# The first 16 modulation blocks as TensorE matmuls in four column groups, and wide weight splits on VectorE

## The chip, the core and the metric

The kernel runs on one core of one Trainium2 chip. The metric is device time in microseconds (us). Three runs of the kernel before gave 1264.8, 1265.66 and 1267.31 us, median 1265.66 us.

The engines are named as in the profile: PE is TensorE's matmul, PEld its weight load, DVE is VectorE, ACT is ScalarE, POOL is GpSimd, SP the engine that issues most DMAs. L183 is line 183 of the kernel before.

## The reference, cut to what matters

One layer over 256 tokens of 1024 channels: a modulation from a conditioning vector, a mixer of three branches, and a mixture of 32 experts. What the change touches is the modulation:

```python
cond = silu(c)                                   # 1024 numbers
mod = cond @ w_ada + b_ada                       # 6 * 1024 numbers
sh_m, sc_m, g_m, sh_f, sc_f, g_f = split(mod, 6)
h = rms_norm(x, norm_mix) * (1 + sc_m) + sh_m    # [256, 1024]
proj = h @ w_in                                  # q, k, v, gates and so on
x = x + g_m * mixer(proj)
h = rms_norm(x, norm_ffn) * (1 + sc_f) + sh_f
x = x + g_f * moe_ffn(h)                         # 32 experts, top 4
```

`mod` is 48 blocks of 128 channels. The first 16 are `sc_m` and `sh_m`; nothing of `proj` can start on a block of 128 channels of `h` before its two blocks of `mod` are there.

## The kernel before, in words

**The first loop** (`branches`, eight passes, one for each block d of 128 channels). A pass loads two tiles `wada` of w_ada (512 KB each) and one tile `wt` of the q, k, v weights (`wqkv`, 896 KB). `ada` makes two columns of `mod`, each by one VectorE instruction (L183) that multiplies a [128, 1024] tile of w_ada, laid out with output channels on partitions, with silu(c) repeated on every partition (`csb`) and sums along the row. `h_chunk` then makes the scale (A, L214), the scaled and shifted block (hd, L217), its rounded part (the ACT cast, L218) and the rest (L219). The weights are split the same way (`split`): ACT rounds to `whi` (L103), POOL or DVE subtracts to get `wlo` (L95), in a wide piece of 1024 columns and one of 768. Three matmuls (`mm3`, L110 to L112) make one product: 24 matmuls in a pass, 18 of them with 512 columns and 6 with 256. Before, all splits of the loop but the last wide one are POOL's.

**silu(c) on every partition** is made by `row_tile` (L489): eight matmuls against the identity and two ACT copies, before the first pass.

**After the loop** come the norms of q and k (`qk_norm`, L275 to L289, on ACT, DVE and PE), the products of the other weights (`proj`, `proj_ch`), a chain of small DVE operations on [128, 4] (`lru_prepare`, sp, L297 to L313), differential attention, sliding-window attention, the recurrence (`lru`), and beside them the other 32 blocks of `mod` by the same VectorE instruction. Then the branches are merged, x is updated, tokens are routed, and the experts stream 12 MB of weights each.

**What sets the order.** Each engine runs its own list in order. The lists are written by a scheduler from the program's dependences and its own priorities, so an edit in the loop also changes the order behind it. Tiles come from pools: 9 tiles for `wada` and others (`p4`), 3 for `wt`, 3 each for `whi` and `wlo`, and 8 banks of PSUM, of which the loop holds 7 for its sums.

Of the kernel before, what the change touches and what calls it, by code (L numbers as in the profile page):

```python
# [27 lines left out]
# the blocks of 128 columns of mod, in the order in which they are computed  # L28
# [3 lines left out]
# those computed beside the chunks of the gates  # L32
ADA = [[10], [11], [12, 13], [14, 15], [16, 17], [18, 19], [20, 21], [22, 23], [], [], [], []]

# columns of the packed per-channel parameters
C_C, C_NM, C_NF, C_CW, C_CB, C_BA, C_BX, C_LAM = 0, 8, 16, 24, 40, 44, 48, 52
C_QG, C_KG, C_SG, C_SQ, C_SK, C_BADA, N_COLS = 56, 57, 58, 59, 60, 61, 109
# columns of the packed rows
R_SINK, R_BR, N_ROWS = 0, 8, 40
# columns of the packed constants  # L40
# [4 lines left out]
class Kernel:  # L45
# [11 lines left out]
    def mm(self):  # L57
        """A bank of PSUM for the products in turn: of two while the other two are held, or of four."""
        self.turn = (self.turn + self.four) % 2
        return self.po() if self.turn else self.psum.tile([128, 512], F32, name="mm", tag="mm", bufs=2)  # L60
# [7 lines left out]
    def weights(self, pool, bufs, after=0):  # L68
        """bufs more tiles for weights, to be used after the next few."""
# [13 lines left out]
    def load_pair(self, srcs):  # L83
        """Two blocks [128, 2, n] in one tile."""
# [6 lines left out]
    def sub_rest(self, lo, x, hi, eng=None):  # L91
        """lo = x - hi, what rounding x to hi has left."""
# [4 lines left out]
    def split(self, w, eng=None):  # L97
        """w as hi + lo, each exact in float32r."""
# [8 lines left out]
    def mm3(self, out, lhs, rhs, start, stop):  # L107
        """out += lhs.T @ rhs, both as (hi, lo)."""
# [52 lines left out]
    def silu_c(self):  # L161
        """Twice silu(c), on every partition."""
# [5 lines left out]
        self.csb = self.row_tile("silu", sc, self.mix)  # L168
        self.mod = self.keep.tile([128, 48], F32, name="mod")

    def ada_load(self, i, first=False):
        ws = []
        for j in range(2):
            ws.append(self.p4("wada") if first else self.p4p.tile([128, D], F32, name="wada", tag="wada", bufs=2))
            self.nc.sync.dma_start(out=ws[j], in_=self.a["wada"][i][:, j * D:(j + 1) * D])
        return ws

    def ada(self, i, ws=None):
        """Columns 2i and 2i + 1 of mod: two blocks of 128 channels."""
# [6 lines left out]
    def normed_T(self, out):  # L186
        """x, rms-normed and transposed, to out: two [128, 4, T]."""
# [21 lines left out]

    def h_chunk(self, x, d):  # L210
        """hhi + hlo [:, d] = channels 128d.. of h, transposed; x: those of normed_T."""
        nc = self.nc
        A = self.A1[:, d:d + 1]
        nc.vector.scalar_tensor_tensor(A, self.mod[:, 2 * d:2 * d + 1], 1.0, self.col(C_NM + d),  # L214
                                       op0=ALU.add, op1=ALU.mult)
# [6 lines left out]
    def bias_tiles(self):  # L222
        """tz[p, head, j]: minus the bias of distance p + j - 127, the masks included."""
# [17 lines left out]
    def tokens_k(self, ps, h, k, hi, lo):  # L241
        """ps[t] += h.T @ w for block k of the channels, w [128, 512] as hi + lo."""
# [4 lines left out]
    def proj(self, ps, h, src):  # L247
        """h.T @ w for 512 columns of w."""
# [11 lines left out]
    def proj_ch(self, i):  # L260
        """Two blocks of 128 channels [128, 2, tokens]."""
# [844 lines left out]
def layout(inp):  # L1106
# [3 lines left out]
    a = {}  # L1110
# [67 lines left out]
```

## Time and profile before

| | |
|---|---|
| median of three runs | 1265.66 us |
| span of the profiled execution | 1268.4 us |
| PE busy | 1136.3 us (90%) |
| DVE busy | 481.9 us (38%) |
| ACT busy | 254.6 us (20%) |
| POOL busy | 126.2 us (10%) |
| moved by DMA | 470.67 MB, mean 371 GB/s |

The page gives no time of the profiled execution but its span, which is 2.7 us above the median of the runs. Shares over the whole span mix stages that have different limits; the table of stages among the rows below keeps them apart. A row of the timeline reads: start, duration, engine, line, operation, result and operands, shapes, and in brackets how long the engine was idle before it and what ended that.

### The profile page before, as it was taken

What the parts mean: (1) busy time and instruction counts of PE and PEld (TensorE: products, weight loads), DVE (VectorE), ACT (ScalarE), POOL (GpSimd) and SP (SyncE); (2) the same over time, 40 slices, a digit from 0 to 9 for tenths busy, and PEclk for the clock granted to TensorE, in tenths of its full rate; (3) what the DMA queues carried; (4) which work ended last, traced back from release to release, by engine and by line L of the source; (5) the groups of instructions that cost most, each with busy time, mean ns of one, the idle gap of its engine ahead of it and who ended that gap; (6) DMA issues with size and microseconds to landing.
All of it is one profiled execution on the core that took longest, in us unless ns stands there. A gap on an engine that the chain in (4) does not pass through costs nothing.

```text
span 1268.4 us, 13945 instructions
## 1 busy us (share of the span) xinstructions
PE 1136.3 (90%) x5559; PEld 543.8 (43%) x5560; DVE 481.9 (38%) x864; ACT 254.6 (20%) x438; POOL 126.2 (10%) x62
## 2 busy tenths in 40 slices
PE   5798998899898899999899898989898989898997
PEld 4577878897334333433332232324232423332232
DVE  6979868774313232322123121303141312121232
ACT  4275647344201010100100000101010100100000
POOL 3643213442000000000000000000000000000000
PEclk8998989899899999999999999999999999999999
DMA  8668456688599999999999999999999999999996
GB/s 336 233 238 299 149 203 217 248 329 366 223 411 421 421 421 420 421 421 421 421 421 421 421 421 421 421 421 421 421 421 420 421 421 421 421 421 421 421 399 253
DMA packets 75084, 470.67 MB, mean 371 GB/s; under 512 B 8464, under 2 KB 10568, under 8 KB 23560
## 3 DMA queue, kind: packets, MB, share of 16 engines
q1 hardware_dynamic: 73544, 467.07, 90.9%
q0 software_dynamic: 464, 1.59, 0.4%
q10 hardware_dynamic: 1008, 1.09, 0.3%
q8 instruction: 45, 0.74, 0.2%
q14 instruction: 23, 0.19, 0.0%
HBM read 468.65 MB, written 1.07 MB: 370 GB/s over the span
## 4 chain that ended last, share of the span: by engine, by line
DMA 50%; PE 35%; DVE 12%; ACT 2%; issue 1%; ACTq 0%; SPq 0%; DVEq 0%
DMA wt<-w1h 30%; DMA wt<-w2h 18%; PE po L879 7%; PE mm L879 6%; PE ps L899 5%; DVE wada L183 4%; PE ps L839 2%; PE ps L912 2%; PE mm L112 2%; PE mm L110 2%; PE mm L111 2%; PE ps L383 1%; DVE wlo L95 1%; DVE A L214 1%; PE po L112 1%
## 5 line engine op out<-in xcount | busy, mean ns | idle before, releaser
L879 PE MATMUL po<-wt,xT 128*64 128x512 f32 x992 | 323.8, 605 | 34.5 <-DMA wt<-w1h 34.5
L879 PE MATMUL mm<-wt,xT 128*64 128x512 f32 x992 | 317.2, 596 | 0.0
L899 PE MATMUL ps<-wt,act 128*64 128x512 f32 x992 | 233.4, 607 | 28.6 <-DMA wt<-w2h 21.8
L905 DVE TENSOR_TENSOR y<-ps,gf 64x512 f32<-64x512 f32 x62 | 42.7, 689 | 380.8 <-PE ps L899 372.0
L879 PEld LDWEIGHTS po<-wt,xT 128*64 128x64 f32 x992 | 78.4, 136 | 176.9 <-DMA wt<-w1h 97.8
L879 PEld LDWEIGHTS mm<-wt,xT 128*64 128x64 f32 x992 | 88.4, 137 | 135.4 <-issue 134.6
L899 PEld LDWEIGHTS ps<-wt,act 128*64 128x64 f32 x992 | 68.2, 138 | 179.8 <-issue 122.2
L95 POOL TENSOR_TENSOR wlo<-wt,whi 128x1024 fp32r<-128x1024 f32 (+1 forms) x43 | 110.7, 2581 | 176.2 <-ACT whi L103 149.3
L809 DVE TENSOR_TENSOR g<-ps,b1t 128x512 f32<-128x512 f32 x31 | 21.4, 692 | 222.3 <-PE ps L806 222.3
L883 ACT COPY hg<-po 128x512 f32<-128x512 f32 x31 | 18.2, 586 | 361.5 <-PE po L879 315.4
L103 ACT CAST whi<-wt 128x1024 fp32r<-128x1024 f32 x72 | 72.7, 1022 | 55.2 <-PE mm L111 31.7
L183 DVE CUSTOM_DVE_ANT_0 wada<-wada,silu,cols 128x1024 f32<-128x1024 f32 x48 | 80.7, 1686 | 2.4 <-DMA wada<-wada 2.3
L112 PE MATMUL mm<-h,wlo 128*128 128x256 f32 x256 | 76.3, 298 | 5.8 <-DVE wlo L95 5.0
L110 PE MATMUL mm<-h,whi 128*128 128x256 f32 x256 | 77.2, 301 | 3.7 <-ACT gl L574 3.7
L111 PE MATMUL mm<-h,whi 128*128 128x256 f32 x256 | 76.5, 299 | 0.0
L912 PE MATMUL ps<-y,swT 128*128 128x512 f32 (+1 forms) x128 | 58.2, 606 | 11.2 <-DVE y L905 11.2
L812 ACT ACTIVATE ps<-g 128x512 f32<-128x512 f32 x31 | 18.6, 601 | 186.1 <-DVE g L810 186.1
L112 PEld LDWEIGHTS mm<-h,wlo 128*128 128x128 f32 x256 | 52.0, 203 | 7.3 <-DVE wlo L95 5.2
L110 PEld LDWEIGHTS mm<-h,whi 128*128 128x128 f32 x256 | 52.2, 204 | 4.6 <-ACT gl L574 3.9
L111 PEld LDWEIGHTS mm<-h,whi 128*128 128x128 f32 x256 | 51.9, 203 | 2.0 <-issue 2.0
L914 DVE TENSOR_TENSOR x<-x,ps 128x512 f32<-128x512 f32 x64 | 43.9, 688 | 15.7 <-PE ps L912 15.7
L95 DVE TENSOR_TENSOR wlo<-wt,whi 128x1024 fp32r<-128x1024 f32 x29 | 39.4, 1360 | 19.5 <-ACT whi L103 19.5
(325 smaller groups left out, 1139.1 us busy)
## 6 DMA issues: line engine op xcount, KB each, us to landing
wt<-w1h SPq DMA_DIRECT2D x248, 1024.0 KB, 19.8
wt<-w2h SPq DMA_DIRECT2D x126, 1024.0 KB, 19.8
wada<-wada SPq DMA_DIRECT2D x48, 512.0 KB, 5.4
wt<-wch SPq DMA_DIRECT2D x16, 1024.0 KB, 5.2
wt<-w1h SPq DMA_DIRECT2D x16, 512.0 KB, 10.8
wt<-wqkv SPq DMA_DIRECT2D x8, 896.0 KB, 4.6
wt<-wbr SPq DMA_DIRECT2D x6, 1024.0 KB, 6.8
wt<-wout SPq DMA_DIRECT2D x4, 1024.0 KB, 14.0
```

The source lines that it names most:

```text
L95: eng.tensor_tensor(lo, x, hi.bitcast(F32), op=ALU.subtract)
L103: self.nc.scalar.copy(hi, w)
L110: nc.tensor.matmul(out, lhs[0], rhs[0], start=start, stop=False)
L111: nc.tensor.matmul(out, lhs[0], rhs[1], start=False, stop=False)
L112: nc.tensor.matmul(out, lhs[1], rhs[0], start=False, stop=stop)
L183: nc.vector.tensor_tensor_reduce(out=w, in0=w, in1=self.csb, scale=0.5, scalar=self.col(C_BADA + c), op0=ALU.mult, op1=ALU.add, accum_out= ...
L839: nc.tensor.matmul(p[:, i * 256:(i + 1) * 256], self.xs[j][:, t, d * 128:(d + 1) * 128], sel[:, t], start=(t + j == 0), stop=(t + j == 2))
L879: nc.tensor.matmul(p[64 * hf:64 * hf + 64], xT[:, k, i * CAP:(i + 1) * CAP], w[:, (2 * j + hf) * 512:(2 * j + hf + 1) * 512], start=(k == ...
L899: nc.tensor.matmul(py[rows[hf]], act[:, (k % 4) * 2 + k // 4, :], w[:, (2 * i + hf) * 512:(2 * i + hf + 1) * 512], start=(k == 0), stop=(k ...
L905: nc.vector.tensor_mul(self.y[r, hf], py[r], self.gf[r, hf * 512:(hf + 1) * 512])
L912: nc.tensor.matmul(p, swT[r, i, t * 128:(t + 1) * 128], self.y[r, hf], start=True, stop=True)
L914: nc.vector.tensor_add(self.x[:, t, s], self.x[:, t, s], p)
```

## The change

`ada` no longer serves the loop. `ada_rows` does: for each of the eight blocks of the contraction one matmul, with silu(c) of that block repeated 32 times as stationary operand and 256 columns of w_ada (both blocks of `mod`) as moving one, in the column group k % 4 of TensorE. The four groups' sums, each on 32 partitions, are copied to SBUF by ACT (`rd`), and two matmuls against a column with four ones (`pick`) add the four and turn them to partitions. One DVE instruction applies the factor 0.5 and the bias with its 1 folded in (`bm`), so that A becomes a plain product. w_ada of the loop is laid out anew (`wad0`). The row tile of silu(c), still needed by the other 32 blocks, is made after the loop. All wide splits of the loop go to DVE, the 768-column ones stay on POOL.

```diff
     def silu_c(self):
         ...
-        self.csb = self.row_tile("silu", sc, self.mix)
+        self.sc = sc
+        self.pick = self.early.tile([128, 1], F32, name="pick")
+        nc.vector.memset(self.pick, 0.0)
+        for j in range(4):
+            nc.vector.memset(self.pick[32 * j:32 * j + 1], 1.0)
+        self.bm = self.early.tile([128, 8, 2], F32, name="bm")
+        b = self.col(C_BADA, 16).rearrange("p (d s) -> p d s", s=2)
+        nc.vector.tensor_scalar(self.bm[:, :, 0], b[:, :, 0], 1.0, None, op0=ALU.add)
+        nc.vector.tensor_copy(self.bm[:, :, 1], b[:, :, 1])
...
+    def ada_rows(self, d, ws):
+        nc = self.nc
+        p = self.ps()
+        for k in range(8):
+            j = k % 4
+            nc.tensor.matmul(p[32 * j:32 * j + 32, :256], self.sc[:, k:k + 1].to_broadcast([128, 32]),
+                             ws[k // 4][:, j * 256:(j + 1) * 256], start=(k < 4), stop=(k >= 4))
+        r = self.mw.tile([128, 256], F32, name="rd")
+        nc.scalar.copy(r, p[:, :256])
+        for i in range(2):
+            nc.tensor.matmul(p[:, 256 + i:257 + i], r[:, i * 128:(i + 1) * 128], self.pick, start=True, stop=True)
+        m = self.mod[:, 2 * d:2 * d + 2]
+        nc.vector.scalar_tensor_tensor(m, p[:, 256:258], 0.5, self.bm[:, d], op0=ALU.mult, op1=ALU.add)
...
     def h_chunk(self, x, d):
-        nc.vector.scalar_tensor_tensor(A, self.mod[:, 2 * d:2 * d + 1], 1.0, self.col(C_NM + d),
-                                       op0=ALU.add, op1=ALU.mult)
+        nc.vector.tensor_mul(A, self.mod[:, 2 * d:2 * d + 1], self.col(C_NM + d))
...
     def branches(self, br, gl):
         ...
-            self.ada(d, w)
+            self.ada_rows(d, w)
             self.h_chunk(gl[d // 4][:, d % 4], d)
-            hi, lo = self.split(wt[:, :1024], nc.vector if d == 7 else nc.gpsimd)
+            hi, lo = self.split(wt[:, :1024], nc.vector)
...
             nc.scalar.copy(dv[:, t], p)
+        self.csb = self.row_tile("silu", self.sc, self.mix)
...
+    a["wad0"] = wa[:, 1::-1].reshape(8, 128, 2, 8, 128).transpose(3, 1, 0, 2, 4).reshape(8, 128, 2048)
```

The change moves instructions in three places that matter below. On PE, at the seam of two passes, the list before goes from the last matmuls of one pass straight to the next (`h_75` and `h_76` are the rounded part of h and its rest):

```order
L110 MATMUL ps<-whi,h_75 128x256
L111 MATMUL ps<-wlo,h_75 128x256
L112 MATMUL ps<-whi,h_76 128x256
L110 MATMUL mm<-whi,h_75 128x512
L111 MATMUL mm<-wlo,h_75 128x512
```

In the changed list the two pick matmuls of the next pass and the eight matmuls of the pass after it stand between:

```order
L110 MATMUL ps<-whi,h_75 128x256
L111 MATMUL ps<-wlo,h_75 128x256
L112 MATMUL ps<-whi,h_76 128x256
L231 MATMUL ps<-pick,rd 128x1 x2
L226 MATMUL ps<-wada,sc 32x256 x8
L110 MATMUL mm<-whi,h_75 128x512
L111 MATMUL mm<-wlo,h_75 128x512
```

The eight use the one bank of PSUM that the loop doesn't hold, so they also wait until DVE has read the pick's result.

On DVE, after the loop, the small operations of the recurrence's parameters (sp) stand before in one piece behind all the norms of q and k but the last two, which come after them:

```order
L227 TENSOR_TENSOR relb<-ps,relb 12x383
L301 TENSOR_SCALAR sp<-sp 128x4
L183 ISA wada,mod<-wada,silu,cols 128x1024
L183 ISA mod 128x1
L95 TENSOR_TENSOR wlo<-wt,whi 128x1024
L302 RECIPROCAL sp<-sp 128x4
L303 TENSOR_TENSOR sp<-sp 128x4
L304 TENSOR_TENSOR sp<-sp 128x4
L305 TENSOR_SCALAR sp<-sp 128x4
L307 SCALAR_TENSOR_TENSOR sp<-sp 128x4 x7
L95 TENSOR_TENSOR wlo<-wt,whi 128x1024
```

In the changed list (its lines are 24 higher) they begin behind the first of the eight norms (q, L307):

```order
L307 TENSOR_TENSOR q<-ps,rs_715 128x512
L303 TENSOR_REDUCE ss_729<-sq 128x8
L95 TENSOR_TENSOR wlo<-wt,whi 128x1024
L192 ISA wada,mod<-wada,silu,cols 128x1024
L192 ISA mod 128x1
L325 TENSOR_SCALAR sp<-sp 128x4
L326 RECIPROCAL sp<-sp 128x4
L327 TENSOR_TENSOR sp<-sp 128x4
L328 TENSOR_TENSOR sp<-sp 128x4
L329 TENSOR_SCALAR sp<-sp 128x4
L158 RECIPROCAL rs_731<-rt 128x8
L331 SCALAR_TENSOR_TENSOR sp<-sp 128x4
```

Five of the 32 later sums stand ahead of the first score before, eight in the changed list.

On DVE, in the recurrence, nine of these sums stand behind the first operation on the gated input (L338) before, six in the changed list (there L362). The end of that stretch before, from the last operation of the recurrence on:

```order
L352 SCALAR_TENSOR_TENSOR xc<-xc,ti 128x1024
L183 ISA wada,mod<-wada,silu,cols 128x1024
L183 ISA mod 128x1
L624 TENSOR_TENSOR wr<-wr,A_2444 128x256
L183 ISA wada,mod<-wada,silu,cols 128x1024
L183 ISA mod 128x1
L95 TENSOR_TENSOR wlo<-wt,whi 128x1024
L183 ISA wada,mod<-wada,silu,cols 128x1024
L183 ISA mod 128x1
L95 TENSOR_TENSOR wlo<-wt,whi 128x1024
```

And in the changed list:

```order
L376 SCALAR_TENSOR_TENSOR xc<-xc,ti 128x1024
L192 ISA wada,mod<-wada,silu,cols 128x1024
L192 ISA mod 128x1
L95 TENSOR_TENSOR wlo<-wt,whi 128x1024
L192 ISA wada,mod<-wada,silu,cols 128x1024
L192 ISA mod 128x1
L95 TENSOR_TENSOR wlo<-wt,whi 128x1024 x2
```

Fewer sums stand ahead of each split there.

## Rows read from the trace of the kernel before

**Rows 1.** Stages: stretch, length, busy us (instructions) by engine, clock, DMA, GB/s.
```profile
20.20:73.85 53.65, 43.73 (x192) 34.02 (x193) 45.94 (x50) 17.56 (x25) 32.41 (x14) 0.96 0.67 239
73.85:116.00 42.15, 36.99 (x240) 32.33 (x239) 35.87 (x71) 28.68 (x48) 17.99 (x12) 0.96 0.82 283
199.00:239.00 40.00, 31.37 (x246) 30.97 (x244) 37.52 (x38) 24.11 (x33) 19.24 (x6) 0.91 0.64 221
326.00:1268.40 942.40, 859.87 (x3790) 300.46 (x3788) 235.91 (x446) 84.36 (x146) 2.52 (x2) 0.99 1.00 411
```

**Rows 2.** Timeline of DVE, one pass of the first loop.
```profile
52.91 1.28 DVE L183 CUSTOM_DVE_ANT_0 wada<-wada,silu,cols 128x1024 f32<-128x1024 f32 x1
...
54.24 2.19 DVE L214 SCALAR_TENSOR_TENSOR A<-mod,cols 128x1 f32<-128x1 f32 x1
56.35 2.94 DVE L183 CUSTOM_DVE_ANT_0 wada<-wada,silu,cols 128x1024 f32<-128x1024 f32 x1
...
59.34 0.41 DVE L217 TENSOR_SCALAR hd<-gl,A,mod 128x256 f32<-128x256 f32 x1
...
60.57 1.28 DVE L183 CUSTOM_DVE_ANT_0 wada<-wada,silu,cols 128x1024 f32<-128x1024 f32 x1
```

**Rows 3.** Timeline of POOL: the last narrow split of the loop.
```profile
69.60 2.15 POOL L95 TENSOR_TENSOR wlo<-wt,whi 128x768 fp32r<-128x768 f32 x1 [3.74 <-ACT whi L103]
```

**Rows 4.** Timeline of ACT ahead of the first pass.
```profile
7.34 0.19 ACT L192 ACTIVATION_READ_ACCUMULATOR xn<-x 128x1 f32 x1
...
9.40 1.28 ACT L157 ACT_TABLE_LOAD   x1
...
12.42 1.76 ACT L103 CAST whi<-wt 128x1024 fp32r<-128x1024 f32 x2
14.09 2.04 ACT L208 COPY gl<-ps 128x512 f32<-128x512 f32 x4
```

**Rows 5.** Timeline of PE: start of passes 0 and 1, two neighbours, what follows the loop.
```profile
20.25 0.80 PE L110 MATMUL mm<-whi,h 128*128 128x512 f32 x1 [6.14 <-ACT h L218]
...
24.46 0.39 PE L111 MATMUL ps<-wlo,h 128*128 128x512 f32 x1
...
24.69 0.40 PE L112 MATMUL ps<-whi,h 128*128 128x512 f32 x1
...
27.03 0.39 PE L110 MATMUL mm<-whi,h 128*128 128x512 f32 x1
...
73.85 0.28 PE L110 MATMUL mm<-h,whi 128*128 128x256 f32 x1
```

**Rows 6.** Timeline of all engines in the router: matmuls like the added ones.
```profile
302.29 0.64 PE L674 MATMUL ps<-x1T,wr 128*32 128x256 f32 x8
...
302.86 0.50 PE L112 MATMUL mm<-whi,m 128*128 128x512 f32 x1
...
311.60 1.05 PE L489 MATMUL po<-kst,mod 128*128 128x128 f32 x8
...
316.55 0.63 PE L683 MATMUL ps<-kst,lgT 128*128 128x32 f32 x4 [0.78 <-ACT lgT L680]
317.22 0.41 DVE L699 SCALAR_TENSOR_TENSOR lg<-ps,rs,lgb 128x32 f32<-128x32 f32 x2 [0.20 <-PE ps L683]
```

**Rows 7.** Timeline of DVE after the loop: a split and an operation on [128, 4].
```profile
73.52 2.57 DVE L95 TENSOR_TENSOR wlo<-wt,whi 128x1024 fp32r<-128x1024 f32 x1 [3.46 <-ACT whi L103]
...
79.75 1.22 DVE L95 TENSOR_TENSOR wlo<-wt,whi 128x1024 fp32r<-128x1024 f32 x1
...
97.92 2.18 DVE L303 TENSOR_TENSOR sp<-sp 128x4 f32<-128x4 f32 x1
```

**Rows 8.** Waits of PE, 73.85 to 116, then 200 to 240: total, times, longest us.
```profile
PE ps L287 <- DVE q L283: 3.6, 1, 3.6
...
PE mm L112 <- DVE wlo L95: 5.0, 1, 5.0
PE mm L110 <- ACT gl L574: 3.7, 1, 3.7
```

More of the change, by code (lines that the diff above doesn't have):

```diff
@@ L174, in ada_load @@
             ws.append(self.p4("wada") if first else self.p4p.tile([128, D], F32, name="wada", tag="wada", bufs=2))
-            self.nc.sync.dma_start(out=ws[j], in_=self.a["wada"][i][:, j * D:(j + 1) * D])
+            src = self.a["wad0"][i] if first else self.a["wada"][i - 8]
+            self.nc.sync.dma_start(out=ws[j], in_=src[:, j * D:(j + 1) * D])
         return ws
@@ L1124, in layout @@
     wa = f["w_ada"][0].reshape(1024, 6, 8, 128)
-    a["wada"] = np.stack([wa[:, s, d].T for s, d in MOD]).reshape(24, 2, 128, 1024).transpose(0, 2, 1, 3) \
-        .reshape(24, 128, 2048)
+    a["wada"] = np.stack([wa[:, s, d].T for s, d in MOD[16:]]).reshape(16, 2, 128, 1024).transpose(0, 2, 1, 3) \
+        .reshape(16, 128, 2048)
+    a["wad0"] = wa[:, 1::-1].reshape(8, 128, 2, 8, 128).transpose(3, 1, 0, 2, 4).reshape(8, 128, 2048)
     oh, neg = _bucket_rows()
```

## The prediction

> **What bounds the kernel now.** I read the table of stages first. From 326 us on, DMA is busy all the time (share 1.00, 411 GB/s) and PE 860 of 942 us: the experts take the time their weights need. What the front of the kernel gains or loses therefore moves the end by as much. The change lies in the front: the loop (20.2 to 73.85 us) has DVE busy 45.9 of 53.7 us and PE 43.7; 199 to 239 us has DVE busy 37.5 of 40 us and PE 31.4 [rows 1].
>
> Then the timelines of the loop. A pass takes 7.66 us (DVE's first sum at 52.91, that of the next pass at 60.57). DVE and POOL take turns: the scale A on [128, 1] lasts 2.19 us and the second sum 2.94 us instead of 1.28, both while POOL splits weights [rows 2]; POOL's 14 instructions of the loop take 32.4 us, 2.31 each [rows 1], two a pass. These 4.6 us and about 3 us of DVE alone make the pass. PE needs less: neighbours of 512 columns start 0.23 us apart [rows 5], 18 of them take 4.2 us, the six of half the columns an estimated 0.7, a pass 4.9 us.
>
> **The change, part by part.**
>
> *The start.* The two ACT copies of silu go from the first passes' path. The table load stood at 9.40 us, and ACT's squares end at 7.53: 1.87 us earlier. The transposes, done at 14.1 when the copies behind them begin [rows 4], end at 12.2. Then the list of ACT has one copy, two casts (1.76), three copies (1.5) and `rd`: one copy from 11.15 us, casts to 13.4, copies to 14.95, `rd` (half a copy's size and more, some 0.35) to 15.3. The picks are like L683: from their start to the DVE operation 0.67 us, and that operation 0.2 [rows 6]: 16.15. POOL's narrow split (2.15, [rows 3]) ends about there too. A alone is taken like that operation, 0.2; hd lasts 0.41 [rows 2], and the ACT cast of the same shape is taken as much: pass 0 of PE starts at 17.2 instead of 20.25.
>
> *The sums on PE.* Four matmuls in four column groups with 256 columns stand in the router: the next instruction of PE starts 0.57 us after them [rows 6]. The same row group has four matmuls of 128 columns one after another, in 1.05 us; four of 256 would then take 2.1. So the groups do run side by side, and with a second round that adds no more than the first, less its start, the eight take some 1.0 us.
>
> *A rule against it.* That row is one change to 32-column groups and back in 0.57 us. The Trainium skill, TensorEngine Tiling (Array Packing), Key Properties, says that changing the tiling mode drains TensorE. By that rule every pass pays two changes more than the columns say; the row has one such pair in it, so the sum above already holds it, and no price of its own is added.
>
> *Seam of two passes.* Two chains run from the end of a pass's matmuls. PE: picks to DVE's result 0.67 + 0.2, then the eight, 1.0: 1.9 us. DVE: POOL's narrow split (2.15) can start once 12 matmuls (2.8) and the cast (0.88) are done, so 5.8 us after the pass's start, 0.9 after its end; A is held until then, as A is held now; then A 0.2, hd 0.41, cast 0.41: 1.92 us. Both agree on 2.0, and 4.9 + 2.0 = 6.9 us a pass. DVE (0.2 + 0.2 + 0.41 + 0.41 + a split of 1.22, [rows 7]) and POOL (2.15) sum to 4.6 us even when they exclude each other, so they no longer bound it. Pass 1 is worse: its eight come behind pass 0 with nothing prepared: 1.0 + 0.35 + 0.67 + 0.2 + 0.2 + 0.41 + 0.41 = 3.2 us.
>
> *A second rule against it.* A split that DVE does while POOL runs lasted 2.57 us, one alone 1.22 [rows 7]. The Trainium skill, SBUF — State Buffer, "SBUF: two separate sides", says that DVE with two SBUF inputs and GpSimd share a port pair as an exclusive lock, and that the loser fully blocks. By that the seven splits moved to DVE could cost 7 x 1.35 = 9.4 us. The trace agrees with the rule, but the moved splits lie beside 4.9 us of matmuls with over 2 us to spare, so the sum takes nothing for them.
>
> *Sum of the loop.* Pass 0 of PE lasted 20.25 to 27.03, 6.8 us [rows 5], its first matmul 0.80 us against 0.39 later, at the lower level of the clock; I keep that. 17.2 + 6.8 + 3.2 = 27.2 for pass 1 (27.03 before); six seams later 27.2 + 6 x 6.9 = 68.6; the last pass ends at 73.5. The row tile of silu comes back: four matmuls of it before the last pass lie where the eight would, the other four (1.05, L489 in [rows 6]) behind it: 74.55 against 73.85 [rows 5]. So the loop, which does 16 DVE sums less, comes out 0.7 us later: passes 0 and 1 overlapped before, and the faster passes only win that back.
>
> *Behind the loop.* The order moves there, and with it three terms. First, PE waits 3.6 us for the norm of the sliding-window q, once [rows 8]. DVE has ahead of it the sp chain, whose members last up to 2.18 us on 4 columns because POOL runs [rows 7]. In the changed list that chain stands earlier, where DVE has room (35.9 of 42.15 us busy, [rows 1], POOL's hold-ups included). I take the 3.6 us as gone. Second, in the recurrence PE waits 5.0 us for a DVE split and 3.7 us for ACT behind DVE [rows 8]; three sums fewer stand there, 3 x 1.28 = 3.8 us [rows 2], and DVE is the bound: -3.8. Third, the three sums stand ahead of or among the first scores instead; two find room, one costs 1.3 us. ACT's list has two table loads (1.28 each, [rows 4]) ahead of the second norm that came later before; the same number in all, of which I let one count: +1.3. On SP, loads of w_ada for the later sums move ahead of the bias rows that the scores need; two of 512 KB at 411 GB/s are 2.5 us, and since the bias is needed only by the first score, behind two more products of weights, I take nothing.
>
> *The sum.* +0.7 - 3.6 - 3.8 + 1.3 + 1.3 = -4.1 us. The span of the profile, 1268.4 us, lies 2.7 us over the median of the runs; a difference of stages carries over, so I set it against the median: 1265.7 - 4.1 = 1261.6 us.
>
> **Bounds.** The eight matmuls: 0.57 us at least (all in one round), 4.2 at most (eight of 256 columns one after another, at the 2.1 for four above). Over seven seams, in which PE's chain is as long as DVE's: 0 to +22. The moved order: from no gain at all (the two terms gone, the two costs of 1.3 kept: +3.3 with the loop) to every PE wait of [rows 8] gone, -12.3. Pass 0 can be up to 1.9 us shorter (6.8 - 4.9), if PE's clock is at its higher level from the start, since sums and picks now come ahead.
>
> **Rivals.**
>
> *No change.* The loop as worked out, and of the two gains behind it one only, or both with the costs doubled: 1263.2 to 1267.5, say 1265. For it: the moved sums must be done somewhere, and DVE is over 80% busy in both stages. Against it: in the last stage DVE does with certainty three sums less behind its first operation.
>
> *Slower: the seam is longer than 2.0 us.* Place: PE between the last matmul of a pass and the first of the next, where four engines hand over in turn (PE, DVE, ACT, PE), which before ran beside matmuls. Price: six seams, 6 us for each us. It decides from where the gain behind the loop is eaten up and 2.5 us more: 6 x (g - 2.0) > 4.1 + 2.5, g above 3.1 us, as when the eight matmuls took 2.2 us or more rather than 1.0. At 3.9 us, 11.4 - 4.1: 1273. For it: no second round on the same groups is in these rows, and pass 1 has 3.2. Against it: the router's row, and all parts of the chain have rows.
>
> *Much faster.* DVE, rid of the sums, lets PE run on through the norms and the recurrence: all 12.3 us of [rows 8] go, the costs vanish: +0.7 - 12.3: 1254. For it: PE is idle 5.2 and 8.6 us in those two stages [rows 1]. Against: ACT and the DMA of weights then come late.
>
> **How the numbers follow.** About 0.2% (2.5 us) is what a measurement can tell from no change. The forecast has 0.45, its own range 1258 to 1264.5; no change 0.25; slower 0.18; much faster 0.12. Of the forecast's 0.45 some 0.06 lie within 2.5 us of the median, of no change's 0.25 some 0.04 beyond it on the slow side: faster 0.45 + 0.12 - 0.06 = 0.51, same 0.25 + 0.06 - 0.04 = 0.27, slower 0.22. The range takes in most of much faster and of no change, and the near part of slower: 1254.5 to 1269.
>
> **What would show it.** In the changed profile: the first matmul of pass 0 near 17.2 us; seams of 2.0 us, with the eight matmuls 1.0 us in all; starts of passes 6.9 us apart with A held by POOL; the first matmul of the next stage near 74.6 us. Behind it no wait of 3.6 us for the norm, and fewer than 8.7 us of waits in the recurrence. Wrong would be: passes at 7.7 us or more; the clock below 2.4 GHz in the loop; a first score no earlier than before; or experts that don't start earlier by what the stages ahead gained.

## Result and the profile after

The changed kernel took 1274.3 us (median of four runs, 1271.0 to 1278.0) beside 1266.5 us of the kernel before (four runs, 1264.8 to 1269.1): ratio 1.0068, interval 1.0043 to 1.0093. It is some 8 us slower, where 1261.6 was forecast.

Executions of one kernel differ by several us, and those with a lower mean granted clock tend to be the longer ones (changed kernel: 1271.0 us at 0.985, 1278.0 at 0.977); totals are therefore compared by medians, profiles by stage, with the clock of the stage beside them where it differs. In every run about 2 us lie outside the span, so the first profile of before (span 1268.4) is of an execution 4 to 5 us above the median. A second profile of before (before_again) is used beside it below.

Lines of the changed kernel are 24 or 25 higher behind `silu_c`. Three stages again, the first two cut at their new ends (answers to [rows 1]; columns as there):

```profile
17.00:77.72 60.72, 54.98 (x348) 42.25 (x349) 20.61 (x47) 25.00 (x38) 16.36 (x10) 0.97 0.74 273
77.72:123.94 46.22, 37.17 (x228) 32.91 (x226) 37.11 (x66) 25.54 (x43) 15.86 (x9) 0.89 0.73 251
...
326.00:1268.90 942.90, 860.20 (x3804) 302.12 (x3803) 237.18 (x452) 84.92 (x147) 2.52 (x2) 0.99 1.00 411
```

In the loop VectorE's busy time has fallen from 45.9 to 20.6 us and POOL's from 32.4 to 16.4, but PE's has risen from 43.7 to 55.0. The stage from the end of the loop to the first score now lasts 46.2 us (before 41.0, from 73.85 to 114.89).

PE's timeline of the start, of one seam and of the last pass (answers to [rows 5]; L215 are the transposes, L226 the eight, L231 the picks, L513 the row tile of silu):

```profile
10.18 3.86 PE L215 MATMUL ps<-kst,xn 128*128 128x128 f32 x16 [10.18 <-DVE xn L209]
...
13.97 1.93 PE L226 MATMUL ps<-wada,sc 128*32 128x256 f32 x16
16.39 0.61 PE L231 MATMUL ps<-pick,rd 128*128 128x1 f32 x4 [0.49 <-ACT rd L229]
18.40 0.50 PE L110 MATMUL mm<-whi,h 128*128 128x512 f32 x1 [1.40 <-ACT h L242]
...
33.62 0.50 PE L231 MATMUL ps<-pick,rd 128*128 128x1 f32 x4
34.45 1.07 PE L226 MATMUL ps<-wada,sc 128*32 128x256 f32 x16 [0.32 <-DVE mod L233]
35.53 0.50 PE L110 MATMUL mm<-whi,h 128*128 128x512 f32 x1
...
72.36 0.50 PE L112 MATMUL mm<-whi,h 128*128 128x512 f32 x1 [1.33 <-DVE xr L571]
...
76.91 1.05 PE L513 MATMUL ps<-kst,sc 128*128 128x128 f32 x8
77.72 0.36 PE L110 MATMUL mm<-h,whi 128*128 128x256 f32 x1
```

The seam reads as forecast: picks at 33.62, a wait of 0.32 us for VectorE, the eight in 1.07 us, the next pass at 35.53, 1.9 us in all; passes 1 to 6 start 6.91 or 6.92 us apart, the last 7.1 behind pass 6. The start and the end don't: pass 0 begins at 18.40, and the next stage at 77.72 instead of 74.55.

VectorE and POOL around the last seam of that loop (answers to [rows 2, 3]):

```profile
69.20 0.16 DVE L239 TENSOR_TENSOR A<-mod,cols 128x1 f32<-128x1 f32 x1
69.40 0.41 DVE L241 TENSOR_SCALAR hd<-gl,A,mod 128x256 f32<-128x256 f32 x1
70.28 2.02 DVE L243 TENSOR_TENSOR h<-hd,h 128x256 fp32r<-128x256 f32 x1 [0.47 <-ACT h L242]
```

```profile
67.25 1.83 POOL L95 TENSOR_TENSOR wlo<-wt,whi 128x768 fp32r<-128x768 f32 x1 [5.09 <-ACT whi L103]
69.56 2.46 POOL L95 TENSOR_TENSOR wlo<-wt,whi 128x1024 fp32r<-128x1024 f32 x1 [0.49 <-ACT whi L103]
```

A, which lasted 2.19 us in [rows 2], lasts 0.16: POOL no longer holds it, though the forecast had it held. But the rest of h of the last pass (L243) needs 2.02 us instead of 0.4, since POOL has begun a split for the next stage at 69.56; that is the 1.33 us that PE waits at 72.36 (the profile names xr, 0.07 us long, that stands right behind L243).

Behind the loop, VectorE's list around the two norms for which PE waits longest (answers to [rows 7]):

```profile
78.52 2.36 DVE L322 TENSOR_SCALAR sp<-lam 128x4 f32<-128x4 f32 x1
...
84.82 1.28 DVE L192 CUSTOM_DVE_ANT_0 wada<-wada,silu,cols 128x1024 f32<-128x1024 f32 x1
...
86.02 2.30 DVE L325 TENSOR_SCALAR sp<-sp 128x4 f32<-128x4 f32 x1
...
89.04 0.19 DVE L158 RECIPROCAL rs<-rt 128x8 f32<-128x8 f32 x1
...
111.88 4.11 DVE L192 CUSTOM_DVE_ANT_0 wada<-wada,silu,cols 128x1024 f32<-128x1024 f32 x1
...
115.92 0.19 DVE L158 RECIPROCAL rs<-rt 128x8 f32<-128x8 f32 x1
```

ACT had finished the input of the reciprocal at 89.04 (rt) at 84.94. It waited 4.1 us behind a sum, an operation of sp that lasted 2.30 us because POOL was in a split (85.96 to 88.30), and four more of sp. The one at 115.92, whose input was there at 112.30, waited behind a sum that lasted 4.11 us instead of 1.28 (POOL was busy from 110.23 to 114.90). PE's waits, from the end of the loop to the first score, then from 200 to 240 us (answers to [rows 8]):

```profile
PE ps L311 <- DVE q L307: 8.5, 2, 4.3
```

```profile
PE mm L112 <- DVE wlo L95: 4.1, 2, 2.2
PE mm L110 <- ACT gl L599: 2.9, 1, 2.9
```

The norms cost PE 8.5 us instead of 3.6 (4.4 with a wait of 0.8 that [rows 8] leave out). In the recurrence 7.0 us are left of 8.7, and 0.4 for a split of POOL's come on top.

### The profile page after: what moved, and what is told of

Same layout as the page of the kernel before. It is cut to its first block, busy times and chain, and to the rows that moved or that the text cites. A ratio compares the mean times of both kernels' runs of the same rounds, so it can differ in the third digit from the quotient of the medians.

```text
span 1268.9 us, 14282 instructions
## 1 busy us (share of the span) xinstructions
PE 1140.6 (90%) x5719; PEld 546.1 (43%) x5720; DVE 449.1 (35%) x854; ACT 260.1 (20%) x446; POOL 103.1 (8%) x55
## 3 DMA queue, kind: packets, MB, share of 16 engines
q1 hardware_dynamic: 73544, 467.07, 90.8%
HBM read 468.65 MB, written 1.07 MB: 370 GB/s over the span
## 4 chain that ended last, share of the span: by engine, by line
DMA 43%; PE 36%; DVE 2%; ACT 0%; issue 0%; SPq 0%; ACTq 0%
DMA wt<-w1h 24%; DMA wt<-w2h 18%; PE po L904 9%; PE mm L904 8%; PE ps L924 7%; PE ps L864 2%; PE ps L937 2%; PE mm L112 1%; PE ps L831 1%; PE mm L110 1%; PE mm L111 1%; PE po L112 1%; PE po L111 1%; PE po L110 1%; DVE y L930 0%; PE ps L893 0%
## 5 line engine op out<-in xcount | busy, mean ns | idle before, releaser
L95 POOL TENSOR_TENSOR wlo<-wt,whi 128x1024 fp32r<-128x1024 f32 (+1 forms) x36 | 87.8, 2438 | 201.1 <-ACT whi L103 190.6
L95 DVE TENSOR_TENSOR wlo<-wt,whi 128x1024 fp32r<-128x1024 f32 x36 | 51.4, 1429 | 17.3 <-ACT whi L103 17.2
L192 DVE CUSTOM_DVE_ANT_0 wada<-wada,silu,cols 128x1024 f32<-128x1024 f32 x32 | 51.0, 1598 | 5.7 <-DMA wada<-wada 5.7
```

The lines of the kernel that those rows point to most:

```text
L95: eng.tensor_tensor(lo, x, hi.bitcast(F32), op=ALU.subtract)
L192: nc.vector.tensor_tensor_reduce(out=w, in0=w, in1=self.csb, scale=0.5, scalar=self.col(C_BADA + c), op0=ALU.mult, op1=ALU.add, accum_out= ...
```

## The experiments

Each ratio is to runs of the kernel before on the same chip. Differences between two kernels are of medians, unless the text says otherwise.

**before_again**: no edit.

> The kernel before, unchanged, for a second profile: the first is of an execution 4 us above the median of its runs. If the clock alone made that (0.90 to 0.91 from 116 to 239 us), this one shows the same waits of PE, the next stage after the loop again at about 74 us, and the router 3 to 5 us earlier than 302 us; if something else did, a stage or a wait differs.

1268.2 us, ratio 1.0008 (0.9989 to 1.0027), clock of the profiled execution 0.979. The next stage begins at 73.94, the first score stands at 115.85, the router's first matmul (L674) at 300.29 against 302.29 in the first profile. PE's waits, from 73.9 to 116 and from 200 to 240:

```profile
PE ps L287 <- DVE q L283: 3.6, 1, 3.6
```

```profile
PE mm L112 <- DVE wlo L95: 4.7, 1, 4.7
PE mm L110 <- ACT gl L574: 3.6, 1, 3.6
```

The waits are those of [rows 8]; the 2 us of the router lie in the attention stages (115.85 to the recurrence: 77.2 us at a clock of 0.93, against 80.1 at 0.89). So the waits and stages that the prediction used hold. One row doesn't: the transposes of the start, 2.07 us in the first profile, take 3.66 here:

```profile
12.14 3.66 PE L206 MATMUL ps<-kst,xn 128*128 128x128 f32 x16 [1.56 <-DVE xn L200]
```

**splits_only**, one half of the change on the kernel before:

```diff
-            hi, lo = self.split(wt[:, :1024], nc.vector if d == 7 else nc.gpsimd)
+            hi, lo = self.split(wt[:, :1024], nc.vector)
```

> The kernel before with one edit: the wide splits of the loop go to VectorE; the sums stay VectorE's, and the order behind the loop stays that of before. Theory A (the 8 us are lost behind the loop, by the new order of VectorE's list around the norms, and the loop itself costs little): none of that loss here; a pass of the loop is VectorE's two sums 2.56, A 0.2, hd 0.41, the rest of h 0.43 and a split 1.22 = 4.8 us, up to 7.0 where POOL's one narrow split (2.15) holds it, against 7.66: 1252 to 1262 us. Theory B (the loop is what costs, above all the splits on VectorE that POOL holds up, 1.35 us each in 7 passes): 1266 + 9 = about 1275 us, no faster than before.

1261.8 us, ratio 0.9971 (0.9957 to 0.9985): faster, as theory A said, at the upper end of its range. The next stage begins at 69.05, 4.8 us earlier. Late passes take 7.17 us; VectorE and POOL in one of them:

```profile
50.82 2.87 DVE L183 CUSTOM_DVE_ANT_0 wada<-wada,silu,cols 128x1024 f32<-128x1024 f32 x1
...
53.62 1.27 DVE L183 CUSTOM_DVE_ANT_0 wada<-wada,silu,cols 128x1024 f32<-128x1024 f32 x1
```

```profile
50.46 2.15 POOL L95 TENSOR_TENSOR wlo<-wt,whi 128x768 fp32r<-128x768 f32 x1 [5.02 <-ACT whi L103]
```

POOL's split ends at 52.61; the sum issued at 50.82 ends 1.08 us after that, in other words it runs when POOL is done, as a sum alone lasts 1.28. The Trainium skill, SBUF — State Buffer, "SBUF: two separate sides", tells of an exclusive lock in which the loser fully blocks; the trace agrees.

**rows_only**, the other half alone:

```diff
-            hi, lo = self.split(wt[:, :1024], nc.vector)
+            hi, lo = self.split(wt[:, :1024], nc.vector if d == 7 else nc.gpsimd)
```

> The changed kernel with one edit: the wide splits of passes 0 to 6 go back to POOL; the matmul sums stay, and so does the changed order behind the loop. Theory A: the loss behind the loop stays whole (two waits of 4.3 us for the norms); the loop's pass is set by PE's chain at the seam, 6.9 us, with POOL's two splits (4.6) inside it: 1271 to 1277 us, like the changed kernel. Theory B: without VectorE's splits the loop is as fast as predicted and the loss is gone: 1266 us or less; if the seam is what costs rather than the splits, 1274.

1285.3 us, ratio 1.0151 (1.0137 to 1.0164). Neither theory said so: passes take 8.60 us, 1.7 more than in the changed kernel, for POOL's wide split now holds the rest of h at each seam:

```profile
48.50 2.12 DVE L243 TENSOR_TENSOR h<-hd,h 128x256 fp32r<-128x256 f32 x1 [0.47 <-ACT h L242]
```

```profile
47.98 2.35 POOL L95 TENSOR_TENSOR wlo<-wt,whi 128x1024 fp32r<-128x1024 f32 x1 [0.48 <-ACT whi L103]
```

So the splits on VectorE are the good half of the change, and the matmul sums, with the order that comes with them, the bad one, by 12 us (1274.3 less 1261.8). Of these, 8.7 us arise ahead of the next stage (77.72 less 69.05).

**sp_late**, the changed kernel with sp behind the last norm:

```diff
-    def lru_prepare(self):
+    def lru_prepare(self, behind):
...
-        nc.sync.dma_start(out=lam, in_=self.a["cols"][:, C_LAM:C_LAM + 4])
+        nc.vector.scalar_tensor_tensor(lam, behind, 0.0, self.col(C_LAM, 4), op0=ALU.mult, op1=ALU.add)
...
-        self.lru_prepare()
+        self.lru_prepare(sq[:, 3, T - 4:])
```

> The changed kernel with one edit: the chain of small operations sp reads its input through one more operation that needs the last norm, so none of it can stand ahead of a norm. Theory A: at the first wait of 4.25 us the held operation (2.30) and the small ones behind it (about 1 us) go, so 3 to 4 us less: about 1270.5 us, with the second wait of 4.28 us (a sum and POOL) left. Theory B: the norms' waits are beside the point: 1274 us, no change from the changed kernel.

1272.3 us, ratio 1.0052 (1.0037 to 1.0067), an interval that overlaps that of the changed kernel. PE's waits for norms fall from 8.5 to 3.9 us, a little more than expected. The first score stands at 113.80 instead of 123.94; about half of these 10 us is PE's busy time, at a clock of 1.00 in this stretch against 0.89. But the last transposes ahead of the sliding-window scores stand at 170.02 instead of 169.19: all of it is given back in the first attention, where PE waits 6.6 us in one piece and its clock is 0.88 against 0.96. VectorE's list there (the sum at 120.35 waits for its load of w_ada, and the scores behind it wait with it):

```profile
120.35 1.28 DVE L192 CUSTOM_DVE_ANT_0 wada<-wada,silu,cols 128x1024 f32<-128x1024 f32 x1 [5.44 <-DMA wada<-wada]
```

**sums_late**, the changed kernel with silu by rows made behind the last norm:

```diff
-        self.csb = self.row_tile("silu", self.sc, self.mix)
...
+        nc.vector.scalar_tensor_tensor(self.sc, sq[:, 3, T - 8:], 0.0, self.sc, op0=ALU.mult, op1=ALU.add)
+        self.csb = self.row_tile("silu", self.sc, self.mix)
         self.diff(dq, dk, dv, br[1])
```

> The changed kernel with one edit: silu(c) by rows is made behind the last norm, so that none of the 32 later sums can stand ahead of a norm (eight do in the changed kernel). Theory A: the second wait (a sum held for 4.11 us) goes, 4.3 us, and 1.3 of the first; but eight sums more (10 us of VectorE) come to the attention stages and the recurrence, which give some of it back: 1269 to 1273 us. Theory B: 1274 us or, as sums pile up behind, up to 1280.

1284.9 us, ratio 1.0132 (1.0099 to 1.0166): beyond both. The executions spread: four at a mean clock of 0.974 to 0.976 took 1284.3 to 1286.2 us, two at 0.983 and 0.989 took 1276.8 and 1272.2. The profile is of the 1276.8 one, so it shows only part of the loss. In it the next stage begins at 74.34, the first score stands at 113.41, but the router at 309.07 instead of 304.41: the sums, put off, stand in the merge of the branches (one at 257.45), each with its load, and hold the gated sums there. Theory A was right on where PE waits (4.2 us for the norms instead of 8.5) and wrong on what it is worth: in these two runs, work put off behind the norms is not won. That made theories C and D.

**small_early**, the changed kernel with sp and lambda (small operations for the differential attention) in the loop's third pass:

```diff
             self.ada_rows(d, w)
+            if d == 2:
+                self.lru_prepare()
+                self.attn_prepare()
...
-        self.attn_prepare()
...
-        self.lru_prepare()
```

> The changed kernel with one edit: the chain sp, and the small operations of lambda with it, are written into the third pass of the loop, where VectorE is idle. Theory C (VectorE's list is full behind the loop; what leaves it for the loop is gained, what is only put off behind the norms comes back later, as sp_late and sums_late showed): the held members of sp (2.36 and 2.30 us) and some 1.5 us of others leave the norms, so their waits fall from 8.5 to 5 us or less and nothing comes back: 1268 to 1271 us. Rival D (behind the norms the loads of w_ada for the later sums come last, as the 5.4 us show that a sum waited for its load in sp_late): whatever is gained at the norms is waited for there: 1272 to 1275 us.

1268.0 us, ratio 1.0033 (1.0013 to 1.0053), 6.3 us less than the changed kernel by the medians, 0.35% or 4.4 us by the ratios (five of the twelve executions took 1270.7 to 1277.0 us), and the two intervals just overlap: theory C, as far as that goes. The loop ends as in the changed kernel (next stage at 77.74); the norms' waits have halved, and the first score stands at 116.80:

```profile
PE ps L311 <- DVE rs L158: 2.7, 2, 1.9
PE ps L311 <- DVE q L307: 2.0, 1, 2.0
```

**all_dve**, the kernel before with all splits of the loop on VectorE:

```diff
-            hi, lo = self.split(wt[:, :1024], nc.vector if d == 7 else nc.gpsimd)
+            hi, lo = self.split(wt[:, :1024], nc.vector)
...
-            hi, lo = self.split(wt[:, 1024:], nc.gpsimd)
+            hi, lo = self.split(wt[:, 1024:], nc.vector)
```

> The kernel before with one edit: all splits of the loop go to VectorE, the narrow ones too, so POOL has no split there. Theory C: no VectorE operation of the loop is held any more; a pass is 2.56 + 0.2 + 0.41 + 0.43 + 1.22 + 0.92 = 5.7 us against 7.17 in splits_only, for about five passes: 7 us less than its 1261.8, some 1255 us. Rival: the narrow split, now in VectorE's list ahead of the next pass's sums, is as long as the hold that it saves: 1260 to 1263 us.

1247.5 us, ratio 0.9851 (0.9826 to 0.9876), twice the expected gain. Every pass from the second on takes 4.91 us, PE's own time; the next stage begins at 59.89, 14 us earlier than before. One pass of VectorE, with nothing held:

```profile
45.63 1.28 DVE L183 CUSTOM_DVE_ANT_0 wada<-wada,silu,cols 128x1024 f32<-128x1024 f32 x1
...
46.83 1.28 DVE L183 CUSTOM_DVE_ANT_0 wada<-wada,silu,cols 128x1024 f32<-128x1024 f32 x1
...
48.04 0.15 DVE L214 SCALAR_TENSOR_TENSOR A<-mod,cols 128x1 f32<-128x1 f32 x1
...
48.56 2.09 DVE L95 TENSOR_TENSOR wlo<-wt,whi 128x1024 fp32r<-128x1024 f32 x2
...
50.90 1.28 DVE L183 CUSTOM_DVE_ANT_0 wada<-wada,silu,cols 128x1024 f32<-128x1024 f32 x1
```

VectorE needs 5.27 us a pass, sums included, and stays ahead of PE over the eight passes from a head start; in a longer loop its 5.27 against PE's 4.91 would tell. The sums weren't too much for it here; POOL's hold was.

**sums_loop**, small_early with 12 of the later sums in the loop:

```diff
+            if d == 1:
+                self.csb = self.row_tile("silu", self.sc, self.mix)
+            if d >= 2:
+                self.ada(6 + d)
...
-        self.csb = self.row_tile("silu", self.sc, self.mix)
...
-            self.ada(8 + i)
```

> small_early with one more edit: 12 of the 32 later sums are written into passes 2 to 7 of the loop, two a pass, and silu(c) by rows into pass 1. Theory C: 12 sums of 1.28 us, 15 us of VectorE, leave the stages behind the loop, of which PE waits for about half: 1258 to 1266 us. Rival D: a pass then loads 2.94 MB, 7.0 us at 421 GB/s against its 6.92, and a sum that waits for its load holds the operations of the seam behind it: passes of 7.5 us or more, 1268 to 1280 us.

1280.6 us, ratio 1.0123 (1.0096 to 1.0149): at the upper end of rival D's range, 0.6 us above it. Passes 3 to 6 take 9.3, 10.9, 10.7 and 12.1 us, and PE waits 13.8 us in the loop for h, `rd` and `mod`. Whether the loads or the sums' places in VectorE's list made these waits, the run doesn't tell.

**rows_all_dve**, the edit that won 14 us on splits_only, on the changed kernel:

```diff
-            hi, lo = self.split(wt[:, 1024:], nc.gpsimd)
+            hi, lo = self.split(wt[:, 1024:], nc.vector)
```

> The changed kernel with one edit: the narrow splits of the loop go to VectorE too, so POOL has no split there. Theory E (in the changed loop the seam of PE's chain sets the pass, picks to VectorE to the eight to h; nothing in it waits for POOL): passes stay at 6.9 us and the time at about 1274, though the same edit took 14 us off splits_only. Theory F (POOL's hold of VectorE, freed in all_dve, is what costs in the changed loop as well): passes of 6 us or less, 1262 to 1268 us.

1273.9 us, ratio 1.0080 (1.0066 to 1.0093): theory E. Passes take 6.85 us; with the sums on PE, POOL's hold is not what bounds passes 1 to 6.

**rows_mid**, the changed kernel with the modulation and h of pass d + 1 in the middle of pass d:

```diff
-            self.ada_rows(d, w)
-            self.h_chunk(gl[d // 4][:, d % 4], d)
...
             self.tokens_k(pq, self.h, d, hi[:, 512:], lo[:, 512:])
+            if d < 7:
+                self.ada_rows(d + 1, w)
+                self.h_chunk(gl[(d + 1) // 4][:, (d + 1) % 4], d + 1)
             hi, lo = self.split(wt[:, 1024:], nc.gpsimd)
```

> The changed kernel with its loop written in another order: the modulation and h of pass d+1 are issued in the middle of pass d, ahead of its narrow split, so that picks and eight stand among the matmuls and not at the seam. Theory E: the seam of 2.0 us goes, and PE's own work is left, 4.9 + 1.07 + 0.5 = 6.5 us a pass or a little under: 7 x 0.4 = 3 us less at the end of the loop, about 1271 us if the order behind stays. Theory F: the pass is held by POOL, no change, 1274 us.

1268.9 us, ratio 1.0034 (1.0013 to 1.0055). The time is 5 us less by the medians, 4.3 by the ratios, and the intervals just overlap. It isn't for the reason given: passes still take 6.85 us. What is won in the loop is pass 1, which starts at 25.89 instead of 28.61, and the last pass, 5.8 us up to the next stage (67.01 to 72.82) instead of 7.4 (70.30 to 77.72). The first score stands 13.7 us earlier (110.28); at the recurrence's first matmul (L330 of before) the two profiles stand level again, at 200.78 and 200.96, with a clock of 0.89 against 0.94 from 108 to 201 us. So part of it is given back in the attention stages, how much the two profiles don't tell. PE in the middle of a pass and at the seam:

```profile
42.59 1.07 PE L226 MATMUL ps<-wada,sc 128*32 128x256 f32 x16
43.59 0.50 PE L110 MATMUL po<-whi,h 128*128 128x512 f32 x1
43.93 0.40 PE L111 MATMUL po<-wlo,h 128*128 128x512 f32 x1
...
44.40 0.50 PE L231 MATMUL ps<-pick,rd 128*128 128x1 f32 x4
44.76 0.48 PE L110 MATMUL po<-whi,h 128*128 128x512 f32 x1
45.08 0.40 PE L111 MATMUL po<-wlo,h 128*128 128x512 f32 x1
```

PE's list of waits is empty in the loop, and the modulation still costs PE 6.85 - 4.91 = 1.94 us a pass: the eight 1.0 (42.59 to 43.59), the picks 0.36 (44.40 to 44.76), some 0.1 ahead of the eight, behind them and behind the picks (the matmul behind the eight holds PE for 0.34 us, 43.59 to 43.93, its neighbours for 0.23), and 0.3 at the start of the next pass. There the load of PE's weights waits for h, which the matmuls' rows don't show:

```profile
46.46 0.19 PEld L110 LDWEIGHTS mm<-whi,h 128*128 128x128 f32 x1 [0.25 <-ACT h L242]
```

So some 1.6 of the 1.9 us at the changed kernel's seam are PE's own work, which this order only moves; most of the rest is still a wait for h. The Trainium skill, TensorEngine Tiling (Array Packing), "Key Properties", has it that a change of the tiling mode drains TensorE. The 0.1 us on either side of the eight (128*32 in the rows) would fit that, but the picks, which keep 128*128, cost as much, so the run doesn't show that it is the drain.

**no_pool**, all_dve with no split of POOL's anywhere:

```diff
-        eng = eng or (self.nc.gpsimd if self.nsub % 2 == 1 else self.nc.vector)
+        eng = eng or self.nc.vector
```

> all_dve with every other split and remainder of POOL's moved to VectorE too, so that POOL holds VectorE nowhere. Behind the loop that is some 17 splits of 1.22 us, 21 us of VectorE, against holds of 1 to 3 us on as many operations. If the holds cost VectorE more than its own splits would: under 1247 us. If less: 1250 to 1260 us, since VectorE is busy 72 of 83 us there already.

1237.9 us, ratio 0.9794 (0.9781 to 0.9808): the fastest, and below the 1247 us from which the expectation told the two cases apart, so the holds cost more than the splits that replace them. Of PE's waits for norms none is left, of those in the recurrence 3.5 us; what it waits for now is the bias, for whose load VectorE waits 6.9 us ahead of the first score:

```profile
101.67 0.29 DVE L385 CUSTOM_DVE_ANT_0 s<-ps,tz 128x128 f32<-128x128 f32 x1 [6.93 <-DMA tz<-scr]
```

**best7**, all_dve with small_early's edit in pass 7:

```diff
+            if d == 7:
+                self.lru_prepare()
+                self.attn_prepare()
...
-        self.attn_prepare()
...
-        self.lru_prepare()
```

> all_dve with the chain sp and lambda written into the last pass of the loop, as small_early has them in the third of the changed kernel. Theory C (what leaves VectorE's list behind the loop for an idle stretch is gained): VectorE ends 2.8 us before the loop's last matmul in all_dve, where these 3 us fit; POOL then holds none of them behind the norms: 2 to 5 us less, 1243 to 1246 us. Rival: they stood behind the norms in all_dve, where PE waits 1.9 us only: no change, 1247 us.

1250.8 us, ratio 0.9893 (0.9874 to 0.9912), 3 us more than all_dve: both expectations missed. Five operations of sp ran into the first split that POOL does for the next stage:

```profile
57.43 3.16 DVE L307 SCALAR_TENSOR_TENSOR sp<-sp 128x4 f32<-128x4 f32 x5
```

The profile doesn't show that they made the loss: the last pass came 5.70 instead of 4.91 us after the one before, ahead of these five operations, and of the 5.5 us that PE waited for norms 5.0 stood behind a sum that waited 1.57 us for its load and a split that POOL held (3.37 us at 89.90).

**mid_small**, the edits of rows_mid and small_early together:

```diff
...
             self.tokens_k(pq, self.h, d, hi[:, 512:], lo[:, 512:])
+            if d == 2:
+                self.lru_prepare()
+                self.attn_prepare()
+            if d < 7:
+                self.ada_rows(d + 1, w)
+                self.h_chunk(gl[(d + 1) // 4][:, (d + 1) % 4], d + 1)
```

> rows_mid with the edit of small_early (the chain sp and lambda in the third pass of the loop). Theory G (the loss is the loop's seam and what stands ahead of the norms, and nothing else): the gains of the two, 5.4 and 6.3 us, add up: 1274.3 - 11.7 = about 1262.6 us, below before. Rival H (VectorE's sums and their loads of w_ada come next): rows_mid's own waits at the norms were 1.5 us only, so the second edit has little left to win: 1266 to 1269 us.

1265.6 us, ratio 0.9999 (0.9987 to 1.0011). By the medians the two edits win 8.7 us of the 11.7 that they win apart, between G and H; by the ratios they win 0.69%, and 0.35 and 0.34 apart, so that they add up as G has it. The runs don't decide between the two. Together the edits make up for the whole loss against before, and leave no gain.

**after_no_pool**, the changed kernel with the edits of rows_all_dve and no_pool:

```diff
-        eng = eng or (self.nc.gpsimd if self.nsub % 2 == 1 else self.nc.vector)
+        eng = eng or self.nc.vector
...
-            hi, lo = self.split(wt[:, 1024:], nc.gpsimd)
+            hi, lo = self.split(wt[:, 1024:], nc.vector)
```

> The changed kernel with all splits and remainders of POOL's on VectorE. If the hold makes the waits at the norms: sp and sums ahead of them last 0.16 and 1.28 us, and the waits fall below 3 us; if the order alone makes them, they stay above 5 us. The loop keeps its 6.85 us a pass, 1.94 more than no_pool's for 8 passes, 15 us: 1237.9 + 12 to 17 = 1250 to 1255 us, so that the change would cost twice as much where POOL holds nothing. If VectorE, rid of 16 sums, gains more behind the loop than that: under 1245 us.

1244.7 us, ratio 0.9838 (0.9816 to 0.9860): not the 1250 to 1255 us expected first, but the last case, under 1245. The waits at the norms are 1.3 us, with sp and sums still standing among the norms (in an order of the scheduler's own, so not operation for operation that of the changed kernel). So the hold made most of the 8.5:

```profile
PE ps L311 <- DVE sp L328: 1.1, 1, 1.1
...
PE ps L311 <- DVE q L307: 0.2, 1, 0.2
```

The next stage begins at 74.45, 14.3 us behind no_pool's 60.14. It is 15.5 us behind at the first score; then some 5 us come back in the attention stages (80.7 against 85.8 us), where no_pool's PE waits 6.7 us behind its bias, and 4.5 in the recurrence (86.4 against 90.8), which leaves 6.0 at the router. The change still costs 6.8 us here (1244.7 less 1237.9; 5.6 by the ratios).

Put together, in us:

| splits in the loop | sums on VectorE | sums on PE |
|---|---|---|
| wide and narrow on POOL | 1265.7 (before) | 1285.3 (rows_only) |
| wide on VectorE | 1261.8 (splits_only) | 1274.3 (the change) |
| all on VectorE | 1247.5 (all_dve) | 1273.9 (rows_all_dve) |
| none on POOL anywhere | 1237.9 (no_pool) | 1244.7 (after_no_pool) |

In each row the sums on PE are slower, by 6.8 to 26 us; in each column the time falls as POOL does less (one step, 1274.3 to 1273.9, is none).

## Why the prediction was wrong

The forecast was made of three stretches. Against the second profile of before they came out so:

| stretch | forecast | measured |
|---|---|---|
| start to the next stage's first matmul | +0.7 | +3.8 (77.72 less 73.94) |
| from there to the first score | -3.6 + 1.3 + 1.3 = -1.0 | +4.3 (46.22 less 41.91) |
| recurrence (L330) to the router (L674) | -3.8 | -3.8 (103.45 less 107.28) |

Between the first score and the recurrence the length doesn't change (77.0 against 77.2, at clocks of 0.98 and 0.93). The sum is 4.1 us at the router and 2.1 at the end of the span by these two profiles, 8 by the medians. The profiled execution of the changed kernel was 3.2 us below its median, that of before_again 2.6 above the median of all runs of before on its chip, which I can't place by stage.

*The step that failed most* is "In the changed list that chain stands earlier, where DVE has room ... I take the 3.6 us as gone". The order ahead shows sp behind the first norm, so seven norms stood behind it. I knew from [rows 7] that a member may last 2.18 us, and from [rows 2] that a sum may last 2.94; I counted room as an average of the stage (35.9 of 42.15 us), where the wait is set by what stands directly ahead of a reciprocal and whether POOL is in a split then. Price: 8.5 us of waits for the 3.6 that were to go. Half of it (the wait at 89.04) is sp's; the other half (115.92) stands behind one of the three sums that moved ahead, for which the forecast had "two find room, one costs 1.3 us". small_early (4.7 us of waits when sp leaves) and after_no_pool (1.3 us when POOL leaves) show both halves of the cause.

*The start*, +1.2 (18.40 for 17.2): I let the transposes end 1.87 us earlier because the table load does. They begin that much earlier (10.18 against 12.03) but take 3.86 us, and I had taken 2.07 from the first profile of before:

```profile
6.71 3.75 PE L489 MATMUL ps<-kst,sc 128*128 128x128 f32 x16 [6.71 <-DMA kst<-consts]
12.03 2.07 PE L206 MATMUL ps<-kst,xn 128*128 128x128 f32 x16 [1.56 <-DVE xn L200]
```

That 2.07 is the exception. Behind the same row tile of silu the transposes take 3.66 us in before_again 3.67 or 3.68 in splits_only, all_dve and no_pool and 3.35 in best7, so it isn't the moved row tile that makes them slow. The larger part of the 1.2 is the first eight, 1.93 us instead of 1.0: in the six kernels with ada_rows whose first eight took 1.07 to 1.14 us, pass 0 began at 17.39 to 17.59; in the four where they took 1.80 to 1.94, at 18.11 to 18.40. What makes them slow in some executions no run shows (ACT's first copy, which the forecast put at 11.15 us without a row for it, began at 11.51); the clock column reads 1.00 from 10.18 to 18.40 us.

*The end of the loop*, +1.7: the last pass took 6.6 us (70.30 to the row tile at 76.91) instead of 4.9, because POOL's first split for the next stage holds the rest of h. I had named the hold for A and not for what stands behind it. Where POOL has no split (after_no_pool), the next stage begins 5.8 us after the last pass (68.63 to 74.45) instead of 7.4.

*What held*: the seam and its terms (1.9 us, 1.07 for the eight), 6.9 us a pass, VectorE and POOL no longer the bound of the loop, and the experts (the router's first matmul to the end of the span lasts 964.5 us, 966.5 in before_again).

*The recurrence* came out at the forecast's number for another reason, in good part luck. Between its first matmul and the router's (columns as in [rows 1]), before_again first:

```profile
193.01:300.29 107.28, 97.78 (x717) 93.61 (x715) 80.01 (x85) 55.86 (x74) 46.83 (x18) 0.95 0.73 278
200.96:304.41 103.45, 94.95 (x709) 90.18 (x707) 76.55 (x77) 55.44 (x74) 45.35 (x18) 0.98 0.72 273
```

VectorE is rid of the three sums (3.5 us), but PE's idle time falls only from 9.5 to 8.5 us. The other 2.8 us are PE's busy time, with 8 of 717 instructions fewer and at a granted clock of 0.98 against 0.95. So VectorE wasn't the bound to the full 3.8 us.

*What the loop's +0.7 hid*: two large terms of opposite sign. The splits alone bring the next stage 4.9 us forward (splits_only, 69.05 against 73.94); the sums on PE, with what moved with them, put it 8.7 back. The prediction had read that POOL's splits make 4.6 of the 7.66 us of a pass, and yet took the sums for the load to be moved; all_dve does the same 16 sums on VectorE and runs at 4.91 us a pass. A time below the 1254 us of the "much faster" rival was reachable, by another edit: leaving the sums where they were.

*The slower rival* named the right sign and the wrong mechanism: the seam of passes 2 to 6 stayed at 2 us. The rule on the shared ports was weighed for the seven moved splits, which indeed last 1.22 us each, unheld; it ought to have been weighed for every VectorE operation that stands ahead of something PE waits for.

*Open*: why three quarters of the difference of the medians don't show between the two profiles; what makes PE's first matmuls slow in some executions; and whether the gains of rows_mid and small_early add up.

## What to carry to other kernels

Before work is moved from an engine that looks full, see how much of its busy time is being held by another engine: here VectorE's sums lasted 2.9 us instead of 1.28, and taking POOL's splits away (ratio 0.979) was worth more than taking the sums away, which made things worse. Where a scheduler rewrites the lists, look in the new order at what stands directly ahead of each operation for which the bound engine waits, at its longest duration in the trace, not at the stage's average room. Small work that nothing waits for soon gained when it moved into an idle stretch well ahead (small_early), cost time in two other places of the loop (sums_loop, best7), and came back as another wait when it was only put off (sp_late, sums_late).

## What was not expected of the hardware

An operation on 128x4 elements with a single tensor operand (L322, 2.36 us; the same line 0.17 in sp_late) is held by POOL's split too, not only the operations with two. POOL's narrow split itself lasts 1.83 us beside an idle VectorE and 2.15 beside a busy one. Where PE changes between the wide matmuls and the eight or the picks, about 0.1 us is lost each time, at three places of a pass. And the row tile's eight matmuls at the start (3.75 us; 2 x 1.05 in [rows 6]) and the transposes behind them (3.66 to 3.68 in four of the profiles, 2.07 in one) can take nearly twice as long as the same work at its fastest, in a stretch whose clock column reads 1.00.
